# A decoder layer in float32 on one core: branch and output projections as seven block products of eight, in one stream with the MLP

## The chip, the core and the metric

The kernel runs on one core of a Trainium2 chip. The time is device microseconds (us) of one execution. The engines are TensorE (PE, matrix products into the eight PSUM banks), VectorE (DVE), ScalarE (ACT), GpSimd (POOL) and SyncE (SP, which here issues most of the transfers between HBM and SBUF). Each engine works through its own instructions in order and waits on semaphores for the others.

## What is computed

One layer of a decoder on x of 1024 tokens by 1024 features, all in float32. Cut to what matters here:

```python
h = rms_norm(x, norm_mix_g)
# three branches from projections of h, each 1024 features wide:
#   y_m: matrix memory, y_d: differential attention, y_c: cross-attention into 256 memory tokens
g_m, g_d, g_c = split(sigmoid(h @ w_gate + b_gate))
merged = g_m * (y_m @ w_proj_m) + g_d * (y_d @ w_proj_d) + g_c * (y_c @ w_proj_c)
x = x + merged @ w_out
h2 = rms_norm(x, norm_mlp_g)
x = x + square(relu(h2 @ w_up)) @ w_down        # 1024 -> 4096 -> 1024
```

## The kernel before

**Products.** Everything on the chip is kept with features on the partitions and the 1024 tokens along the row. A float32 operand is split into a rounded high part and the rest (`split`, `split2`: a copy on ACT that rounds, then a subtraction on DVE), and a product is three matmuls, high by high, high by low and low by high (`mm3`). So one product of 128 x 128 weights with 512 tokens is three matmuls of 512 columns.

**Stages.** `run` computes the three branches and the sigmoid gates (`gate_steps`; the gate products are used to fill PE while branch work waits), and stores the branch outputs (`store_y`, in `yd`) and the gates to HBM. Then `tail` runs three stages:

1. *Branch projections*, for branches c, m and d: `k_tiles` loads the branch output as eight tiles of 128 features and splits them; for each of four groups of 256 output features `group` runs 2 x 2 tiles x 8 steps x 3 = 96 matmuls. `merge` multiplies each result tile by its gate and adds it to the sum over branches (on POOL for the second branch).
2. *Output projection*: the same `group` four times on the merged tiles. `res` adds x, stores the new x, adds up the squares for the next norm (POOL), and stores the scaled tile for the next stage.
3. *Up projection* (`wino`), and then `down`: these already work with block products. Weights and operand are cut in quarters (two feature halves by two output halves for the weights, two feature halves by two token halves for the operand). Seven products of sums of quarters (`PROD`) stand in for eight products of quarters.

**A unit of block products.** Take 256 output features and all tokens. For each of the four steps of 256 input features, seven `mm3` go into seven PSUM banks: 4 x 7 x 3 = 84 matmuls. The weights of a step come in as four quarters; POOL makes four sums (`wino_s`, L1124 to L1127), ACT and DVE split all seven (`wsp`, tile `wo`, L104 and L105). The operand's sums are made by `wino_t` (L1106 to L1109, three on DVE and one on POOL) and split into a tile of seven blocks (`xo`, or `xd` in the down projection). At the end of the unit `combine` adds the seven PSUM banks up to the four result tiles (L1179 to L1185, on DVE), and `use_up` finishes them. The next unit's first product goes to the eighth bank, the others into banks as `combine` empties them.

**Order.** In these stages the instructions of PE, DVE and ACT are kept in program order (`InOrder`, `pinned`); the weight split of a step is issued two to three steps ahead of its products. A wait at the head of an engine's queue holds everything behind it. Where nothing is pinned, the framework's planner orders the instructions by its own estimates.

**Changes of stage.** The up projection starts with a special order, `runs`: its first unit is computed in two halves around the second. The down projection has its own pools, and 28 accumulators; there four operand tiles stay in SBUF and each pass takes one new.

## Time and profile before

| | us |
|---|---|
| runs (three) | 2285.44, 2285.45, 2289.59; median 2285.45 |
| span of the profiled execution | 2287.7 |
| PE busy | 2203.0 (96% of the span) |
| DVE busy | 1388.2 (61%) |
| ACT busy | 1012.3 (44%) |
| POOL busy | 543.9 (24%) |

The profile comes from an execution of its own. Its span runs from the first to the last instruction; the page gives no other time for that execution. Busy shares are averages over stages that have different limits: the branches run to about 1193 us, the rest of the gates to about 1286, the branch projections to 1547, the output projection to 1640, the up projection to 1953 and the down projection to the end. So each stage is read by itself.

### The profile page before, as it was taken

The page shows a single profiled execution, that of the slowest core. Times are in us where ns is not written, and L with a number is a line of the kernel's source. Part 1 is how long each engine was busy: PE and PEld are TensorE (multiplying, and loading weights), DVE is VectorE, ACT ScalarE, POOL GpSimd, SP SyncE. Part 2 cuts the span into 40 slices and gives each one's busy share as a digit, 9 for nine tenths or more (in the row PEclk, how much of TensorE's full clock was granted, in tenths as well). Part 3 has the DMA queues.
Part 4 walks back from the last instruction along what each step waited for, and adds up shares of the span by engine and source line. Part 5 has one row for each costly group of instructions (what it writes and reads, how often), then busy time and mean ns, then how long its engine had stood idle before and what let it go on. Part 6 is the DMA issues. An engine that isn't in the chain of part 4 may idle for free.

```text
span 2287.7 us, 30578 instructions
## 1 busy us (share of the span) xinstructions
PE 2203.0 (96%) x11222; PEld 1884.3 (82%) x11222; DVE 1388.2 (61%) x2627; ACT 1012.3 (44%) x1994; POOL 543.9 (24%) x696
## 2 busy tenths in 40 slices
PE   7999999999999999999899999999999999899998
PEld 5788789888898999999787888887787888688777
DVE  6636457552147777777652123454598777856678
ACT  6533445543246666666453112223445444543332
POOL 2100000000011111111000002201576665565553
PEclk9999999999999999999999999999999999999999
DMA  6023212201311110011134225435525444844434
GB/s 242 19 79 102 88 44 83 83 24 62 98 58 33 38 37 24 19 38 33 42 113 168 101 90 174 134 115 173 195 99 204 152 153 148 319 164 152 139 128 166
DMA packets 113781, 247.90 MB, mean 108 GB/s; under 512 B 11065, under 2 KB 19550, under 8 KB 111582
## 3 DMA queue, kind: packets, MB, share of 16 engines
q1 hardware_dynamic: 111326, 233.36, 30.4%
q10 hardware_dynamic: 2304, 12.58, 1.3%
q8 instruction: 88, 1.44, 0.3%
q14 instruction: 63, 0.52, 0.1%
HBM read 178.76 MB, written 67.14 MB: 107 GB/s over the span
## 4 chain that ended last, share of the span: by engine, by line
PE 70%; DVE 14%; DMA 7%; ACT 5%; issue 3%; POOL 2%; SPq 0%; ACTq 0%; DVEq 0%; POOLq 0%
PE mm L91 43%; PE p L91 18%; PE sc L91 4%; ACT dpe L987 2%; PE po L91 2%; DVE sc L979 1%; PE tp L94 1%; DMA wraw<-in_wdown 1%; DMA raw<-in_wd 1%; DVE wo L105 1%; DVE w L112 1%; DVE dpe L1000 1%; DVE daT L112 1%; DVE dq L867 1%; DMA raw<-in_wgate 1%
## 5 line engine op out<-in xcount | busy, mean ns | idle before, releaser
L91 PE MATMUL mm<-w,hT 128*128 128x384 f32 (+3 forms) x2496 | 474.0, 331 | 13.7 <-DVE dq L867 9.0
L91 PE MATMUL mm<-hT,w 128*128 128x512 f32 x1920 | 471.0, 400 | 8.2 <-ACT w L111 5.2
L91 PEld LDWEIGHTS mm<-hT,w 128*128 128x128 f32 x1920 | 360.1, 191 | 84.9 <-ACT w L111 5.8
L91 PEld LDWEIGHTS mm<-w,hT 128*128 128x128 f32 x2496 | 387.4, 189 | 33.3 <-DVE dq L867 13.7
L91 PE MATMUL p<-xd,wo 128*128 128x512 f32 x1344 | 314.1, 395 | 16.2 <-DVE acc L1543 8.5
L91 PEld LDWEIGHTS p<-xd,wo 128*128 128x128 f32 x1344 | 253.9, 190 | 76.3 <-DVE acc L1543 12.4
L91 PE MATMUL p<-xo,wo 128*128 128x512 f32 x1344 | 307.5, 390 | 3.2 <-DVE st L1397 1.8
L91 PEld LDWEIGHTS p<-xo,wo 128*128 128x128 f32 x1344 | 251.4, 188 | 57.9 <-ACT pt L1210 2.2
L112 DVE TENSOR_TENSOR w<-raw,w 128x256 fp32r<-128x256 f32 (+3 forms) x304 | 172.9, 589 | 162.4 <-ACT w L111 161.2
L91 PE MATMUL mm<-kt,w 128*128 128x512 f32 x1152 | 261.3, 389 | 0.0
L91 PEld LDWEIGHTS mm<-kt,w 128*128 128x128 f32 x1152 | 216.2, 188 | 45.0 <-DVE w L112 0.2
L111 ACT CAST w<-raw 128x256 fp32r<-128x256 f32 (+3 forms) x304 | 154.3, 532 | 193.5 <-PE mm L91 112.8
L104 ACT CAST wo<-wraw 128x896 fp32r<-128x896 f32 x122 | 114.8, 942 | 187.7 <-PE p L91 121.9
L105 DVE TENSOR_TENSOR wo<-wraw,wo 128x896 fp32r<-128x896 f32 x122 | 146.2, 1213 | 51.3 <-ACT wo L104 51.1
L1124 POOL TENSOR_TENSOR wraw<-wraw 128x128 f32<-128x128 f32 x128 | 100.9, 788 | 207.3 <-DMA wraw<-in_wdown 132.5
L987 ACT ACTIVATE dpe<-sc,dst,drr 128x256 f32<-128x256 f32 (+7 forms) x128 | 106.6, 833 | 94.0 <-DVE dst L983 92.0
L105 DVE TENSOR_TENSOR xd<-xd 128x1536 fp32r<-128x1536 f32 (+2 forms) x36 | 69.2, 1929 | 69.4 <-ACT xd L104 69.3
L979 DVE CUSTOM_DVE_ANT_0 sc<-sc,tmask 128x256 f32<-128x256 f32 (+7 forms) x128 | 96.9, 757 | 16.5 <-PE sc L91 16.5
L1125 POOL TENSOR_TENSOR wraw<-wraw 128x128 f32<-128x128 f32 x128 | 100.9, 788 | 0.0
L127 POOL TENSOR_SCALAR drr<-drr 128x16 f32<-128x16 f32 x16 | 3.6, 222 | 397.4 <-DVE drr L935 397.4
L1126 POOL TENSOR_TENSOR wraw<-wraw 128x128 f32<-128x128 f32 x128 | 90.7, 708 | 0.0
L127 POOL TENSOR_SCALAR hss<-hss 128x4 f32<-128x4 f32 x8 | 3.3, 409 | 356.2 <-ACT mscr L747 237.6
(319 smaller groups left out, 3084.9 us busy)
## 6 DMA issues: line engine op xcount, KB each, us to landing
wraw<-in_wup SPq DMA_DIRECT2D x64, 256.0 KB, 3.1
r_d<-xts SPq DMA_DIRECT2D x16, 1024.0 KB, 4.2
wraw<-in_wdown SPq DMA_DIRECT2D x64, 256.0 KB, 2.8
xd<-r_d SPq DMA_DIRECT2D x19, 768.0 KB, 6.9
xd<-r_d SPq DMA_DIRECT2D x14, 1024.0 KB, 5.9
raw<-in_wgate SPq DMA_DIRECT2D x48, 256.0 KB, 2.8
gates<-gt SPq DMA_DIRECT2D x48, 256.0 KB, 2.0
raw<-in_wd SPq DMA_DIRECT2D x32, 384.0 KB, 3.2
```

Of the source, the lines that this page charges most:

```text
L91: self.pin(self.nc.tensor.matmul(out, l, r, start=start, stop=stop))
L94: self.pin(self.nc.tensor.transpose(out, x, self.ident))
L104: self.A.copy(hi, src)
L105: self.V.tensor_sub(lo, src, f32(hi))
L111: nc.scalar.copy(hi, src)
L112: nc.vector.tensor_sub(lo, src, f32(hi))
L867: V.scalar_tensor_tensor(out=qT[lo, c], in0=pt[lo], scalar=self.gd[lo], in1=f32(qT[lo, c]), op0=ALU.mult, op1=ALU.subtract)
L979: V.tensor_tensor_reduce(out=sc[:, 0:n], in0=sc[:, 0:n], in1=self.tmask[:, D - n : D], scale=1.0, scalar=-3.0e38, op0=ALU.add, op1=ALU.max ...
L987: nc.scalar.activation(pe[c][:, 0:n], sc[:, 0:n], AF.Exp, bias=t8[:, 2 + c : 3 + c], scale=rr[:, i, c : c + 1], accum_out=t8[:, 4 + c : 5 ...
L1124: G.tensor_add(r[:, 4], r[:, 0], r[:, 3])
L1125: G.tensor_sub(r[:, 5], r[:, 4], r[:, 1])
L1126: G.tensor_sub(r[:, 6], r[:, 1], r[:, 0])
```

## The change

The branch projections and the output projection become units of the kind that the up projection has. Units 0 to 3 are branch c, 4 to 7 branch m, 8 to 11 branch d, 12 to 15 the output projection and 16 to 31 the up projection; 128 steps of four to a unit run in one loop, and `down` goes on with the same rings: two weight tiles of two steps each (`w_load`, `w_sum`), three split weight tiles (`w_split`), five operand tiles X (four in `down`). The special order at the start of the up projection is gone.

The operand's block sums of the branch outputs are made while the branches run: `keep_y` stores the quarters, and `finish_y` makes four sums in place on POOL and stores them. For branch c, `cross` does this from HBM during branch m. Operand tiles then come ready from HBM and only need the split. The first three, and the first weights, are loaded and split while the last gates run.

The merge of a branch now works on the four result tiles of a unit, with a running sum that goes to HBM and back (`pd`) between the branches. The operands of the output and up projections are made from the unit just finished; one in four goes through HBM (`od`, `ud`). In one loop, all of DVE, ACT and POOL are kept in program order. The list `early` holds what is issued ahead of a step's weight work, `late` what follows it, and `switch` sets these for a change of branch.

The diff, cut to its core:

```diff
+    def quarters(self, b, t):
+        V, G = self.V, self.G
+        G.tensor_sub(t[:, 0], b[:, 2], b[:, 0])
+        V.tensor_sub(t[:, 1], b[:, 0], b[:, 1])
+        V.tensor_sub(t[:, 2], b[:, 2], t[:, 1])
+        V.tensor_sub(t[:, 3], b[:, 3], t[:, 2])
...
+    def finish_y(self, b, kp, t):
+        self.quarters_in_place(t)
+        self.nc.sync.dma_start(self.yx[b][kp, :, 3:7], t)
...
+        def cross(kp):
+            y = pool.tile([P, 4, 512], F32, tag="yc", name=self.name("ycq"))
+            nc.sync.dma_start(y[:, 0], self.yc0[kp])
+            nc.sync.dma_start(y[:, 1:4], self.yx[2][kp, :, 0:3])
+            self.finish_y(2, kp, y)
...
+        for kp in range(4):
+            add(170 + 90 * kp, cross, kp)
...
+    def w_side(self, n):
+        self.w_split(n + 2)
+        if n % 2:
+            self.w_load((n + 5) // 2)
+        else:
+            self.w_sum(n // 2 + 2)
...
+            def use_branch(u, cs):
+                bi, g = divmod(u, 4)
+                t = gt[u]
+                for i in (1, 3, 2, 0):
+                    V.scalar_tensor_tensor(out=t[:, i], in0=t[:, i], scalar=1.0, in1=cs[i], op0=ALU.add, op1=ALU.mult)
+                    if bi:
+                        G.tensor_add(bt[u][:, i], bt[u][:, i], t[:, i])
+                yield
+                if bi < 2:
+                    A.dma_start(self.pd[g], bt[u] if bi else t)
+                else:
+                    t_make(u)
+                yield
+            def use_out(u, cs):
...
+                for i in (1, 3, 2, 0):
+                    V.scalar_tensor_tensor(out=x[:, i], in0=cs[i], scalar=0.5, in1=x[:, i], op0=ALU.mult, op1=ALU.add)
...
+                t_make(u)
+                for i in range(4):
...
+                        A.activation(q, x[:, i], AF.Square)
+                        G.tensor_add(ssq[:, s], ssq[:, s], q)
+                yield
...
+            def switch(N, i, srcs):
+                s = lambda k: (i + k) % 5
+                if 0 in srcs:
+                    LA(N - 13, lambda: self.x_load(i, s(0), srcs[0]))
+                    LA(N - 10, lambda: sp_(i, 0))
+                    LA(N - 9, lambda: sp_(i, 1))
+                if 1 in srcs:
+                    LA(N - 4, lambda: self.x_load(i + 1, s(1), srcs[1]))
+                    LA(N - 2, lambda: (sp_(i + 1, 0), sp_(i + 1, 1)))
...
+            for N, i, u, d in ((48, 12, 8, self.od), (64, 16, 12, self.ud)):
+                LA(N - 11, lambda u=u, i=i: make(u, i, i % 5, (0,)))
+                LA(N - 10, lambda u=u, i=i: make(u, i, i % 5, (1,)))
+                EA(N - 6, lambda u=u, d=d: keep(u + 1, d))
+                switch(N, i, {1: d})
+                LA(N - 2, lambda u=u, i=i: make(u + 2, i + 2, (i + 2) % 5, (0, 1)))
+                LA(N + 1, lambda u=u, i=i: make(u + 3, i + 3, (i + 3) % 5, (0, 1)))
...
+            for n in range(128):
+                u, kp = divmod(n, 4)
...
+                for j, (l, q) in enumerate(self.PROD):
+                    self.mm3(ps[j], (w[:, l, 0], w[:, l, 1]), (x[:, q, 0], x[:, q, 1]), kp == 0, kp == 3)
...
+                for f in early.pop(n, []):
+                    f()
+                self.w_side(n)
+                for f in late.pop(n, []):
+                    f()
+                if kp == 3:
+                    cs = self.combine(ps, True)
+                    g = (use_branch if u < 12 else use_out if u < 16 else use_up)(u, cs)
+                    step = lambda g=g: next(g, None)
+                    for k in range(3):
+                        early.setdefault(n + 1 + k, []).insert(0, step)
...
-            self.tail()
+                        self.tail_open(ct)
+                        tasks = self.tail_tasks()
+                        for i, _ in enumerate(self.gates):
+                            if i % 6 == 1:
+                                next(tasks, lambda: None)()
+                        for f in tasks:
+                            f()
+            self.tail(ct)
...
-    nc = bacc.Bacc("TRN2", target_bir_lowering=False, num_devices=1)
+    nc = bacc.Bacc("TRN2", target_bir_lowering=False, num_devices=1, dynamic_dma_scratch_size=1024)
```

The weights of the four projections are laid out in quarters on the host, as those of the MLP were. `split2` is used for all splits of the stream.

769 lines of the change are left out of this document (328 added, 441 removed).

## The prediction

> **What bounds the kernel now.** I read the page first: span, busy shares, chain of waits.
>
> ```profile
> span 2287.7 us, 30578 instructions
> PE 2203.0 (96%) x11222; PEld 1884.3 (82%) x11222; DVE 1388.2 (61%) x2627; ACT 1012.3 (44%) x1994; POOL 543.9 (24%) x696
> ...
> PE 70%; DVE 14%; DMA 7%; ACT 5%; issue 3%; POOL 2%; SPq 0%; ACTq 0%; DVEq 0%; POOLq 0%
> ...
> L91 PE MATMUL mm<-kt,w 128*128 128x512 f32 x1152 | 261.3, 389 | 0.0
> ```
>
> TensorE (PE) is the bound, and the three branch projections (the last row) are its cleanest stretch: 1152 matmuls in 261.3 us with no idle time, so a matmul of 512 columns costs 261.3/1152 = 0.2268 us of PE. The 389 ns is one matmul's latency; they overlap. Next, when the stages start and end, by tile, and how busy each engine is in some stretches (columns: length, then busy time and count of PE, PEld, DVE, ACT, POOL, the granted clock, DMA).
>
> ```profile
> L91 PE MATMUL mm<-kt,w x1152: 388/389/411, 1286.4 to 1547.3; 128*128 128x512 f32 x192
> L91 PE MATMUL p<-xo,wo x1344: 387/389/505, 1639.9 to 1953.1; 128*128 128x512 f32 x192
> L91 PE MATMUL p<-xd,wo x1344: 387/389/797, 1953.3 to 2283.3; 128*128 128x512 f32 x192
> ```
>
> ```profile
> 1547.50:1639.90 92.40, 89.29 (x385) 73.08 (x385) 39.23 (x38) 32.23 (x42) 25.82 (x20) 0.98 0.57 189
> 1639.90:1953.30 313.40, 310.17 (x1378) 255.21 (x1377) 257.10 (x304) 152.78 (x218) 201.34 (x267) 1.00 0.45 160
> 1940.00:1990.00 50.00, 42.58 (x166) 33.01 (x165) 42.01 (x40) 27.71 (x31) 25.46 (x30) 0.91 0.87 314
> 1655.00:1700.00 45.00, 45.00 (x208) 37.57 (x207) 44.56 (x55) 20.92 (x29) 38.17 (x47) 1.00 0.28 99
> 1245.00:1560.00 315.00, 315.00 (x1385) 260.61 (x1385) 111.50 (x133) 62.73 (x75) 28.21 (x29) 1.00 0.36 120
> ```
>
> By these rows the output projection takes 92.4 us for 384 matmuls (87.1), so it loses 5.3; the up projection takes 313.4 for 1344 (304.8), 8.6 over. In 1940 to 1990, at the change to the down projection, 166 matmuls ran where 50/0.2268 = 220 fit: 12.3 us lost. Two more things count below. While the branches are projected VectorE (DVE) is busy 111.5 of 315 us: there is room. From 1655 to 1700 it is busy 44.56 of 45 us with GpSimd (POOL) at 38.17, and PE still loses nothing: that is how full the pair can be.
>
> **What is removed.** A projection group goes from 96 matmuls to 4 x 7 x 3 = 84 (a unit), in 16 groups: 192 matmuls, 192 x 0.2268 = **-43.5 us**. All of it is on the path, as PE is. A unit then lasts 84 x 0.2268 = 19.05 us. The separate starts of the output and up stages go too: -5.3, and of the 8.6 what the 32 small matmuls of the row statistics don't use.
>
> ```profile
> L91 PE MATMUL px<-dg,ones 128*128 128x128 f32 x16 | 2.1, 274 | 0.0
> L91 PE MATMUL px<-ones,ssq 128*128 128x1 f32 x16 | 1.8, 245 | 0.0
> ```
>
> They stay (3.9), so -4.7.
>
> **What is added, and on which engines.** Each unit of projection now does what a unit of the up projection does: four weight splits (w_split, one DVE subtraction of 896), the seven adds out of PSUM (combine), eight POOL operations of 256 (w_sum). In use_branch and use_out come four operations of 512 whose inputs are both in SBUF, as combine leaves its results there. Units 4 to 11 add four POOL adds of 512, units 8 to 15 the block sums (three of 512 on DVE, one on POOL), units 12 to 15 up to four POOL adds for the row statistics. And each operand tile X is split once: 1536 and 2048 on DVE. Prices, first of DVE and POOL alone, then where they meet:
>
> ```profile
> L105 DVE TENSOR_TENSOR wo<-wraw,wo x122: 1075/1196/1377, 1651.9 to 2273.9; 128x896 fp32r<-128x896 f32 x122
> L112 DVE TENSOR_TENSOR xo<-xr,xo x4: 1746/1754/2009, 1591.0 to 1660.1; 128x1536 fp32r<-128x1536 f32 x4
> L112 DVE TENSOR_TENSOR xo<-xts,xo x4: 2279/2339/2542, 1593.3 to 1663.3; 128x2048 fp32r<-128x2048 f32 x4
> L1328 DVE TENSOR_TENSOR gl<-mg,gl x16: 691/692/943, 1485.9 to 1548.5; 128x512 f32<-128x512 f32 x16
> L1326 POOL TENSOR_TENSOR mg<-mg,gl x16: 1282/1284/1298, 1394.2 to 1461.5; 128x512 f32<-128x512 f32 x16
> ```
>
> ```profile
> 1681.61 3.67 DVE L1214 TENSOR_TENSOR pt<-pt,p 128x512 f32<-128x512 f32 x6
> ...
> 1687.08 0.94 DVE L1179 TENSOR_TENSOR pt<-pt,pt 128x512 f32<-128x512 f32 x1
> 1687.95 0.94 DVE L1108 TENSOR_TENSOR xts<-rq,xts 128x512 f32<-128x512 f32 x1
> 1688.81 0.95 DVE L1180 TENSOR_TENSOR pt<-pt,pt 128x512 f32<-128x512 f32 x1
> ...
> 1693.56 0.68 DVE L1184 TENSOR_TENSOR pt<-pt,pt 128x512 f32<-128x512 f32 x1
> 1694.17 0.68 DVE L1183 TENSOR_TENSOR pt<-pt,pt 128x512 f32<-128x512 f32 x1
> ```
>
> ```profile
> 1682.41 0.46 POOL L1125 TENSOR_TENSOR wraw<-wraw 128x128 f32<-128x128 f32 x1
> 1682.94 0.46 POOL L1127 TENSOR_TENSOR wraw<-wraw 128x128 f32<-128x128 f32 x1
> 1683.36 1.30 POOL L1107 TENSOR_TENSOR xts<-rq 128x512 f32<-128x512 f32 x1
> ...
> 1687.44 0.90 POOL L1125 TENSOR_TENSOR wraw<-wraw 128x128 f32<-128x128 f32 x1
> 1688.42 0.79 POOL L1127 TENSOR_TENSOR wraw<-wraw 128x128 f32<-128x128 f32 x1
> ```
>
> ```profile
> 1807.83 0.69 DVE L1106 TENSOR_TENSOR xts<-rq 128x512 f32<-128x512 f32 x1 [0.74 <-ACT rq L1383]
> 1808.56 1.67 DVE L1108 TENSOR_TENSOR xts<-rq,xts 128x512 f32<-128x512 f32 x1
> ```
>
> Read them so. While DVE adds out of PSUM (1681.61, six in 3.67 us, 0.61 each) POOL runs at its own speed (0.46 and 1.30). When DVE has both inputs in SBUF and POOL works too, they take turns: DVE starts one every 0.87 us (1687.08, 1687.95, 1688.81) where alone it starts one every 0.61 (1693.56, 1694.17), so a POOL operation of 128 costs DVE 0.26. One of 512 costs 1.10: the two DVE operations from 1807.83 to 1810.23 take 2.40 where 0.61 + 0.69 would do. On the line between, one of 256 costs 0.54 (an estimate; two of 128 would be 0.52). Starts follow 0.08 us closer than the shown durations (0.69 against 0.61), so 896 counts 1.00, and a tile X 1.67 + 2.20 = 3.87.
>
> The Trainium skill, page "SBUF — State Buffer", section "Who interferes with whom", says that a DVE instruction with two SBUF inputs contends with a GpSimd instruction that reads SBUF, and that the loser fully blocks. It speaks against this change, which puts just such work on both. That they exclude each other the rows bear out; that a whole profiled duration is blocked they don't: 0.69 + 0.46 = 1.15 would be the step, and it is 0.87. What the sum would be by it is among the rivals.
>
> DVE's time in a unit, without X: 7 x 0.61 + 4 x 0.61 + 4 x 1.00 = 10.7. POOL charges it 8 x 0.54 = 4.3, and 1.10 for each operation of 512. Some of that lies beneath the PSUM adds: in the stretch at 1681.61 POOL filled 2.7 of 3.67 us, so I let three quarters of 4.3 (3.2) hide; the bounds are all and none.
> - Units 0 to 3: 10.7 + 4.3 - 3.2 = 11.8, with X at most 17.4. PE hides it.
> - Units 4 to 7 (X: 6.1, 3.9, 0, 5.5): 10.7 + 8.7 - 3.2 = 16.2. Over 19.05 by 3.2, 1.0, 0, 2.7.
> - Units 8 to 11 (X: 6.1, 3.9, 0, 7.7): 12.5 + 9.8 - 3.2 = 19.1. Over by 6.2, 4.0, 0.1, 7.9.
> - Units 12 to 15 (X: 3.9, 3.9, 0, 7.7): the same, 2.2 less in unit 12. Over by 1.7, 3.9, 0.1, 7.8.
> - Unit 16, with the remains of 15 and one X: 3.9. Later up units have no more than before: nothing.
>
> Together 42.5. The weight ring enters two steps (9.5 us) ahead; I count half of that as cover, so **+38 us**. All hidden: 25; none hidden: 80.
>
> **Smaller terms.** The fourth X of the first stage can load only when the gates have left their memory; it is needed 3 x 4.76 = 14.3 us later.
>
> ```profile
> DMA to landing us min/median/max: 4.4/6.6/13.7
> L1384 ACTq DMA_DIRECT2D r_d<-rq x16: 326/327/348, 1681.1 to 1966.4; - x16
> POOL wraw L1124 <- DMA wraw<-in_wup: 63.9, 24, 19.2
> ```
>
> X tiles (xd, first row) land in 4.4 to 13.7 us, and split plus ACT copy take some 6: between 0 and 6, I take **+3**. At the change to the down projection X 20 loads early, but 21 to 23 still stand with the last combine in DVE's queue (3 x 3.87 + 4.3 + 2.4 + 1.8 = 20 us), and the weight split of step 130 behind them has 9.5 us: of the 12.3 lost now I take **-5** (0 to -12). In the branches POOL does 48 block sums of 512 in place (cross, finish_y): 48 x 1.10 = 53 us of DVE at most, of which the chain of waits has 14%: 0 to 7, **+4**. The hss and drr statistics queue behind up to four of them (5.1 us) and are wanted a chunk later. On ACT's queue a store of pd waits for POOL's adds, and the next weight cast stands behind it; this is inside the excess, since that cast feeds DVE. ACT's 32 more issues of 0.33 lie in its idle 56%. On SP the finish_y stores wait for POOL with weight loads behind them: hidden by loads a group ahead, else the 5 us of one finish each.
>
> Sum: 2287.7 - 43.5 - 5.3 - 4.7 + 38 + 3 - 5 + 4 = **2274.2** for the profiled execution. The page gives no time beside its span, and the runs' median, 2285.45, lies 2.3 below it, so I predict **2272**.
>
> **Rivals.**
> - The pair does not bind (its excess is absorbed by the rings): 38 becomes 0, 2236 or 2234 in the runs. For it: 1655 to 1700, DVE full, PE whole. Against: there the work of both just fitted; here twelve units in a row exceed it, and rings of two or three tiles carry no more than 10 us.
> - **Slower**: POOL blocks DVE for its whole duration (0.73 for 256, 1.28 for 512, from 0.46 and 1.28). Each unit from 4 on gains some 2.3 us, the excess is 71 - 5 = 66: 2302, in the runs 2300. With nothing hidden beneath the adds, because POOL then waits for its weights (63.9 us of such waits now), 80: 2314. It decides from an excess of 43.5 + 5.3 + 4.7 + 5 - 3 - 4 = 51.5. For it: DVE is in order, and X splits stand ahead of weight splits. Against: the step of 0.87. The skill's sentence on full blocking is this rival.
> - No change: an excess of 47 to 56, for instance because the three X loads at a change of branch land late (13.7 us) and hold DVE's queue some 5 us at each of two changes: 2283 and up.
>
> **Chances.** Forecast (excess 25 to 47) 0.38; not bound 0.17; no change 0.15; slower 0.30. No change means within 0.2% (4.6 us), about what a measurement tells apart. Faster 0.55, same 0.15, slower 0.30. The range runs from a little above the unbound case to near "nothing hidden": 2240 to 2312; the forecast's own is 2257 to 2280.
>
> **What would show it.** Units 0 to 3 near 19.05 us each, without idle PE; units 4 to 7 near 21, 8 to 15 near 23, with PE waiting for DVE (combine, weight split) and DVE over 95% busy there; up units at 19.05 again; under 12 us lost at the start of the down projection; branches before 1286 as now. It is wrong if units 8 to 15 keep 19.05, if PE waits there for DMA instead, or if the branches are over 7 us longer.

## The result and the profile after

The changed kernel takes 2389.86 us (median of 4 runs, 2386.07 to 2390.72) against 2287.52 for the kernel before in the same series (2285.44 to 2293.31): a ratio of 1.0435, 95% interval 1.0409 to 1.0461. The forecast was 2272, its range ended at 2312. The profiled execution took 2386.07, its span 2384.1, so the difference to explain is 2384.1 - 2287.7 = 96.4 us.

The page of the changed kernel first: span, busy shares, the matmuls of the stream (both projections and the whole MLP are one group now) and the weights' block sums on POOL.

```profile
span 2384.1 us, 29987 instructions
PE 2212.2 (93%) x11030; PEld 1862.6 (78%) x11030; DVE 1585.5 (67%) x2747; ACT 1058.3 (44%) x2015; POOL 672.0 (28%) x635
...
L80 PE MATMUL p<-x,wo 128*128 128x512 f32 x4032 | 976.0, 403 | 87.6 <-DVE wo L56 25.2
...
L56 POOL TENSOR_TENSOR wraw<-wraw 128x256 f32<-128x256 f32 x376 | 379.0, 1030 | 538.1 <-DMA wraw<-in_wup 159.0
```

PE has 11030 matmuls in place of 11222, the 192 that the change removes, and yet it is busy 9 us longer and stands 87.6 us ahead of matmuls of the stream. By tile, the first row gives the start of the stream; the second is the copy with which ScalarE opens each unit's combine, 32 in all. The difference of two starts of that copy is taken below as the length of a unit; where the copy is late in ACT's queue and PE is not, one unit looks longer and the next shorter.

```profile
L80 PE MATMUL p<-x,wo x4032: 387/393/797, 1308.8 to 2379.3; 128*128 128x512 f32 x192
L56 ACT COPY u<-p x32: 567/579/587, 1324.3 to 2051.8; 128x512 f32<-128x512 f32 x32
```

The stream begins at 1308.8, where the first branch product began at 1286.4: **+22.4** before the first product that the change touches. The down projection begins near 2055.7, so 32 units take 746.9 where branches, output and up projections took 666.9: **+80**. The down projection and the end take 328.4 against 334.4: **-6**. Together 96.4.

A unit without idle PE would be 19.05 us. Units 1 to 3 took 67.4 (10 over), units 4 to 17 372.7 (**106 over**, of which unit 17 alone, which took 35.7, has 17), units 18 to 30 262.5, 20.2 each (15 over), unit 31 24.9 (6 over). The stretches of the changed kernel, units 4 to 7, 8 to 11, 12 to 15, 16 and 17, and 18 to 30, then units 4 to 17 as a whole (length, then busy time and count of PE, PEld, DVE, ACT and POOL, granted clock, DMA share, GB/s):

```profile
1391.70:1487.10 95.40, 83.28 (x336) 63.92 (x336) 71.88 (x68) 29.67 (x30) 47.69 (x44) 0.96 0.64 233
1487.10:1588.60 101.50, 86.65 (x336) 66.06 (x336) 90.05 (x77) 31.33 (x30) 70.21 (x50) 0.93 0.54 189
1588.60:1699.20 110.60, 90.10 (x336) 67.99 (x336) 89.40 (x81) 42.39 (x47) 65.70 (x51) 0.88 0.43 148
1699.20:1764.50 65.30, 50.38 (x183) 38.98 (x183) 41.07 (x49) 21.53 (x29) 26.19 (x23) 0.82 0.24 84
1764.50:2026.90 262.40, 255.35 (x1095) 203.88 (x1094) 200.86 (x235) 117.00 (x172) 105.73 (x117) 1.00 0.40 145
...
1391.64:1764.38 372.74, 310.29 (x1189) 236.87 (x1190) 292.40 (x273) 124.87 (x132) 209.79 (x165) 0.90 0.48 170
```

The last row is the one to read twice. In units 4 to 17 **no engine is full**: PE 83%, DVE 78%, POOL 56%, ACT 34%, DMA 48%. DVE, which the prediction held to be the bound, stands for 80 of the 372.7 us. What PE waits for in 1380 to 1765 (us in total, times, longest):

```profile
PE p L80 <- DVE wo L56: 17.2, 16, 3.4
PE p L80 <- DVE c L56: 13.8, 7, 4.4
PE p L80 <- ACT u L56: 12.3, 4, 5.1
PE p L80 <- ACT wo L56: 10.3, 6, 5.9
```

And DVE and ACT in the same stretch, their largest waits:

```profile
DVE wo L56 <- ACT wo L56: 50.1, 18, 6.7
```

```profile
ACT wo L56 <- POOL wraw L56: 66.8, 12, 11.6
ACT wo L56 <- PE p L80: 39.2, 8, 12.7
ACT b L56 <- issue: 35.5, 3, 12.7
ACT wo L56 <- POOL b L56: 29.4, 4, 9.1
ACT q L56 <- POOL ssq_rb L56: 21.2, 10, 6.1
```

PE waits for a weight split (wo on DVE) or for a combine (u on ACT, c on DVE); DVE's weight split waits for ACT's cast; ACT's cast waits for POOL's sums, or for an instruction ahead of it in ACT's queue. The chain has one more link, outside these engines. In the same stretch POOL's sums wait for the weight loads, 106 us over the four weight tensors, half of it for those of branch m (the row below). On SP's queue, which issues these loads, a weight load waits until DVE's split has freed the raw weight tile, of which there are two (121.6 us), and the gate loads ahead of it for POOL's adds (91.3 us). Such a wait is a loss only where the sums then come late: in units 18 to 30 POOL waits for weight loads 127.8 us, and PE stands 7.

```profile
POOL wraw L56 <- DMA wraw<-in_wpm: 52.1, 5, 12.1
```

One unit of this, the change from unit 15 to 16, in the timelines of DVE, ACT and PE (start, us, in brackets the idle time before and its releaser):

```profile
1691.16 2.44 DVE L56 TENSOR_TENSOR wo<-wraw,wo 128x896 fp32r<-128x896 f32 x2 [6.67 <-ACT wo L56]
1693.52 3.95 DVE L56 TENSOR_TENSOR x<-x 128x1536 fp32r<-128x1536 f32 x2
1697.39 2.30 DVE L56 TENSOR_TENSOR x<-b,x 128x1536 fp32r<-128x1536 f32 x1
1699.62 2.82 DVE L56 TENSOR_TENSOR x<-t,x 128x2048 fp32r<-128x2048 f32 x1
1702.36 1.61 DVE L56 TENSOR_TENSOR wo<-wraw,wo 128x896 fp32r<-128x896 f32 x1
1703.89 0.67 DVE L56 TENSOR_TENSOR c<-u,p 128x512 f32<-128x512 f32 x1
...
1715.40 1.46 DVE L56 TENSOR_TENSOR wo<-wraw,wo 128x896 fp32r<-128x896 f32 x1 [2.54 <-ACT wo L56]
```

```profile
1689.67 0.63 ACT L56 ACTIVATE q<-g 128x512 f32<-128x512 f32 x1 [1.37 <-POOL ssq_rb L56]
1690.21 1.76 ACT L56 CAST wo<-wraw 128x896 fp32r<-128x896 f32 x2
...
1699.08 0.57 ACT L56 COPY u<-p 128x512 f32<-128x512 f32 x1
1712.34 1.15 ACT L56 ACTIVATE b<-g,vec 128x1024 f32<-128x1024 f32 x1 [12.69 <-issue]
...
1714.44 0.93 ACT L56 CAST wo<-wraw 128x896 fp32r<-128x896 f32 x1
```

```profile
1691.18 1.22 PE L80 MATMUL p<-x,wo 128*128 128x512 f32 x2 [5.90 <-ACT wo L56]
...
1704.62 11.53 PE L80 MATMUL p<-x,wo 128*128 128x512 f32 x38 [3.96 <-DVE c L56]
```

Read it downward. ACT squares for the row statistics and waits for POOL to free the tile of squares (1.37); the two weight casts behind the square start at 1690.21, so DVE, which stood 6.67, and PE, which stood 5.90, go on at 1691.2. Then DVE splits X for 9 us; ACT has opened the combine at 1699.08, but DVE comes to it only at 1703.89, and PE stands 3.96 for a bank. Now ACT stands 12.69 (the row names no releaser; DVE makes g, from which b is made, from 1709.04 to 1712.86); only then does it make b, and behind b the next weight cast at 1714.44, for which DVE has stood 2.54 by 1715.40. At each moment one engine works for the others.

Unit 17 is long for a reason of its own. Its work holds the row statistics of the MLP's norm, and in ACT's fixed order the copy of the row factor stands until PE has made it; the next weight casts, at 1754.77, are behind that copy and what follows from it:

```profile
1744.43 0.59 ACT L56 COPY ssq_rb<-px 128x512 f32<-128x512 f32 x1 [15.15 <-PE px L80]
```

In the kernel before the two such copies stood 0 and 2.34 us.

### The profile page after: what moved, and what is told of

It reads as the page before. It is cut to its first block, busy times and chain, and to the rows that moved or that the text cites. A ratio compares the mean times of both kernels' runs of the same rounds, so it can differ in the third digit from the quotient of the medians.

```text
span 2384.1 us, 29987 instructions
## 1 busy us (share of the span) xinstructions
PE 2212.2 (93%) x11030; PEld 1862.6 (78%) x11030; DVE 1585.5 (67%) x2747; ACT 1058.3 (44%) x2015; POOL 672.0 (28%) x635
## 5 line engine op out<-in xcount | busy, mean ns | idle before, releaser
L80 PE MATMUL p<-x,wo 128*128 128x512 f32 x4032 | 976.0, 403 | 87.6 <-DVE wo L56 25.2
L80 PEld LDWEIGHTS p<-x,wo 128*128 128x128 f32 x4032 | 770.7, 193 | 291.3 <-DVE wo L56 41.0
L56 POOL TENSOR_TENSOR wraw<-wraw 128x256 f32<-128x256 f32 x376 | 379.0, 1030 | 538.1 <-DMA wraw<-in_wup 159.0
L56 DVE TENSOR_TENSOR wo<-wraw,wo 128x896 fp32r<-128x896 f32 x190 | 238.2, 1263 | 191.5 <-ACT wo L56 181.3
L56 DVE TENSOR_TENSOR x<-x 128x1536 fp32r<-128x1536 f32 (+1 forms) x60 | 129.3, 2161 | 20.1 <-ACT x L56 20.0
L56 DVE TENSOR_TENSOR u<-u,p 128x512 f32<-128x512 f32 x160 | 107.1, 686 | 14.1 <-DVE u L56 0.9
L56 ACT CAST x<-x 128x1536 fp32r<-128x1536 f32 (+1 forms) x60 | 101.0, 1691 | 15.3 <-DMA x<-y 14.3
L56 DVE TENSOR_TENSOR acc<-acc,p 128x512 f32<-128x512 f32 x100 | 67.2, 685 | 30.3 <-PE p L80 29.4
L80 PEld LDWEIGHTS po<-dv,daT 128*128 128x128 f32 x576 | 75.6, 193 | 13.8 <-DVE daT L101 12.3
L80 PE MATMUL po<-dv,daT 128*128 128x256 f32 x576 | 78.4, 280 | 7.0 <-DVE daT L101 6.9
```

Of the source, the lines that this page charges most:

```text
L56: return self.tc.keep_in_program_order(f(*a, **k))
L80: self.pin(self.nc.tensor.matmul(out, l, r, start=start, stop=stop))
```

## The experiments

All kernels below are the changed one with the edit shown. Unit lengths are read as above. Each of e1 to e15 was run once, e16 four times. The kernel before took 2282 to 2295 us in these comparisons, so the stretches inside one profile decide rather than differences of a few us in the whole. How well a stretch repeats is seen where the edit lies ahead of the stream (e4, e7, e10, e15): units 4 to 17 took 370.6 to 376.1 there, units 18 to 30 261.7 to 262.7. The table collects what was measured: the time, the start of the first branch product, the length of the two groups of units, and the share of units 4 to 17 in which VectorE is busy.

| kernel | us | first product | units 4-17 | units 18-30 | DVE busy in 4-17 |
|---|---|---|---|---|---|
| changed | 2389.86 | 1308.8 | 372.7 | 262.5 | 78% |
| e1 adds on VectorE | 2371.08 | 1312.3 | 359.6 | 257.1 | 82% |
| e2 weight split first | 2380.51 | 1307.1 | 375.8 | 252.9 | 77% |
| e3 weight sums left out | 2341.17 | 1308.6 | 335.4 | 259.4 | 81% |
| e4 cross placed later | 2384.66 | 1307.1 | 373.0 | 262.2 | 78% |
| e5 no GpSimd | 2330.62 | 1307.5 | 328.9 | 255.0 | 81% |
| e6 stores on SyncE | 2379.65 | 1310.6 | 368.0 | 262.1 | 81% |
| e7 cross pinned | 2408.57 | 1326.5 | 376.1 | 261.7 | 78% |
| e8 e5 and no splits of X | 2298.67 | 1311.0 | 300.8 | 254.4 | 71% |
| e9 combine first | 2417.01 | 1309.5 | 390.8 | 275.9 | 71% |
| e10 no early sums | 2363.13 | 1285.8 | 372.2 | 261.7 | 79% |
| e11 lead of three | 2448.42 | 1310.8 | 396.8 | 295.0 | 75% |
| e12 e1, e9 and e11 | 2353.81 | 1308.8 | 345.5 | 262.4 | 85% |
| e13 two of three matmuls | 2378.53 | 1314.0 | 371.6 | 264.1 | 79% |
| e14 e12, weight sums on VectorE | 2439.45 | 1306.6 | 373.0 | 309.1 | 83% |
| e14b e1, e2 in up, sums on VectorE | 2429.14 | 1312.9 | 384.8 | 284.0 | 80% |
| e15 cross in the last branch | 2380.58 | 1304.6 | 370.6 | 262.7 | 79% |
| e16 e12 and e15 | 2344.49 | 1307.1 | 341.9 | 260.5 | 86% |

**Is it the pair of VectorE and GpSimd?** The first theory is the prediction's slower rival: the two engines keep each other off SBUF for longer than was counted.

```diff
-        G.tensor_sub(t[:, 0], b[:, 2], b[:, 0])
+        V.tensor_sub(t[:, 0], b[:, 2], b[:, 0])
...
-                        G.tensor_add(bt[u][:, i], bt[u][:, i], t[:, i])
+                        V.tensor_add(bt[u][:, i], bt[u][:, i], t[:, i])
...
-                        G.tensor_add(ssq[:, s], ssq[:, s], q)
+                        V.tensor_add(ssq[:, s], ssq[:, s], q)
```

> The changed kernel with 70 operations of 512 moved from GpSimd to VectorE: the 32 adds of the branch sum, the 24 first block sums of a result and the 14 adds for the row statistics. All else as in the changed kernel (span 2384.1 us; units 4 to 17 take 373 us). Theory 1, the shared port: such an operation costs VectorE 1.10 us while GpSimd does it and 0.61 when VectorE does it, so units 4 to 17 get shorter, by 20 to 40 us. Theory 2, VectorE simply has too much to do in order and GpSimd is no hindrance: 70 x 0.61 = 43 us more on VectorE, so longer by up to 40 us.

Measured: units 4 to 17 13 us shorter, the up units 5 (their one POOL operation of 512 per unit moved too). The sign is that of theory 1, the pair; the size is below its 20.

```diff
-        if i < len(self.wsrc):
+        if i < 2:
             r, G = self.raws[i], self.G
```

> The changed kernel without the weight sums on GpSimd (the four sums of each weight pair are made only for the first two pairs and what they left is used for all others; the weight loads and splits stay). Theory 1, the shared port: GpSimd's charge on VectorE falls by 4.3 us in every unit, so units 4 to 17 get some 50 us shorter and the up units go to 19.1 (15 us). Theory 3, queue order: the splits still stand behind the finishing of a unit; the up units stay near 20 and units 4 to 17 gain less than 20.

Measured: 37 us off units 4 to 17, between the two theories, and 3 off the up units, as theory 3 said. The edit takes away POOL's meetings with DVE and also the wait of ACT's cast for the sums, so the 37 are not contention alone. Both edits of e1 and e3 together:

> Both edits of before together: the 70 operations of 512 (branch adds, first block sum, sums of squares) on VectorE, and the weights' block sums left out after the first two pairs (the tiles of the first pairs stand in, so the products of the later weights are wrong numbers; loads, splits and matmuls stay). GpSimd has next to nothing to do in units 4 to 17. Those took 372.8 us in the changed kernel, 359.7 with the operations moved, 335.5 with the sums left out; 266.7 without an idle TensorE. Theory A (VectorE and GpSimd hold each other up, and this is the excess): the two gains add up or more, 4 to 17 at 322 or less, the whole at 2328 or less. Theory B (what is left is the order of the queues, the splits of X ahead of the combine, and VectorE's own work): the 70 operations are simply more work for VectorE, 4 to 17 stay at 333 to 350, the whole at 2339 to 2357.

Measured: 328.9, between the two theories; the gains (13 and 37) come to 44 together, less than their sum. The window of units 4 to 17 in that kernel shows DVE still idle 62 us with POOL out of the way:

```profile
1388.22:1717.13 328.91, 293.51 (x1189) 229.23 (x1190) 267.23 (x328) 125.46 (x132) 1.85 (x2) 0.94 0.53 190
```

So POOL's work is a part of the 106 us, and not the larger one: with all of it gone from POOL 62 stay. (VectorE has the moved operations to do in e5; what the stretch would take without them was not run.) ACT's casts, which wait for the weight loads themselves once the sums are gone, stood 9.7 us for them in e5 in 1380 to 1720; a third raw weight tile was not tried. What a meeting costs can be read from one operation, DVE's weight split, in the changed kernel and then in e5 (groups with shapes kept apart, 1388 to 1762):

```profile
L56 DVE TENSOR_TENSOR wo<-wraw,wo 128x896 fp32r<-128x896 f32 x56 | 81.5, 1468 | 50.7 <-ACT wo L56 47.4 <-issue 3.2
```

```profile
L56 DVE TENSOR_TENSOR wo<-wraw,wo 128x896 fp32r<-128x896 f32 x64 | 68.8, 1087 | 34.6 <-ACT wo L56 33.9
```

1.468 against 1.087. Over all of DVE's work in units 4 to 17: 292.4 busy in the changed kernel; in e5 267.2, of which the 328 - 273 = 55 moved operations are 55 x 0.69 = 38; 292.4 - (267.2 - 38) = 63 us of contention.

**Weights ahead of the unit's other work.** In each step w_side was called after the pieces of work kept in `early`; here before them.

```diff
-                for f in early.pop(n, []):
-                    f()
-                self.w_side(n)
+                self.w_side(n)
+                for f in early.pop(n, []):
+                    f()
```

> The changed kernel with only the order of issue changed: in each step the weight work stands ahead of the steps that finish the unit before. Theory 3, queue order (the weight copy on ScalarE and its subtraction on VectorE stand behind the finishing of a unit and come too late for TensorE): the up units go from 20.2 to about 19.1 us (15 us in all), the units 4 to 17 gain 20 us or more. Theory 1, the shared port: the work is the same, so units 4 to 17 change by less than 8 us in all, and the up units stay at 20.2.

Measured: up units 252.9, 10 us shorter, units 4 to 17 3 us longer (no more than the spread above). So the 15 us of the up units are for two thirds the order of ScalarE's and VectorE's queues: the cast for the next weights stood behind ReLU and square of the last unit.

**Stores.** ScalarE's queue issues the stores of the stream, and a store waits for its data.

```diff
-                A.dma_start(d[:, 0:3], bt[u][:, 1:4])
+                nc.sync.dma_start(d[:, 0:3], bt[u][:, 1:4])
... (the same for the other five stores of the stream)
```

> All stores of the stream issued by SyncE's queue in place of ScalarE's. Theory A (a store that waits for VectorE's last block sum holds ScalarE's queue, and with it the copy that opens the next combine): units 4 to 17 shrink by 20 us or more, the whole at 2366 or less. Theory B (ScalarE only waits for what it would wait for anyway): units 4 to 17 within 8 us of 372.8, the whole at 2378 to 2394. Theory C (on SyncE's queue the waiting stores hold back the loads of X and of the weights): longer than 2394.

Measured: 368.0, 5 us shorter: theory B. At most these 5 us of ScalarE's idle time are the stores'.

**The splits of X.** e5, and the splits left out from the sixth input on:

```diff
         t = self.X[i]
-        self.split2(t[:, s, 0], t[:, s, 1], f32(t[:, s, 1]))
+        if not 5 <= i < 20:
+            self.split2(t[:, s, 0], t[:, s, 1], f32(t[:, s, 1]))
```

> As the kernel without GpSimd's work in the loop (operations of 512 on VectorE, weight sums left out after the first two pairs), and also without the splits of X after the first five inputs of products: the loads of X stay, TensorE multiplies by the tiles of earlier X, so the output is wrong numbers from there on. Theory A (the splits, which stand ahead of the next combine in VectorE's and ScalarE's queues, are the rest of the excess): units 4 to 17 at 267 to 285 us, the whole at 2270 to 2300. Theory B (the rest is the gates, block sums, stores and sums of squares, which stay): units 4 to 17 at 300 or more, the whole over 2305.

Measured: 300.8, 28 us less than e5, and 2298.67 for the whole: by the stretch theory B, by the whole theory A. Neither holds alone: the splits are 28 of the 62 us that e5 has over its matmuls, 34 stay. Most of those lie in unit 8 (28.8 us, 9.7 over) and in units 16 and 17 (54.3, 16.2 over; the copy of the row factor stands 12.99 us there).

**Order alone.** The combine is issued ahead of the splits that stood before it.

```diff
+                if kp == 3:
+                    cs = self.combine(ps, True)
+                    ... (the steps of the unit's further work, as before)
                 for f in early.pop(n, []):
                     f()
                 self.w_side(n)
                 for f in late.pop(n, []):
                     f()
-                if kp == 3:
-                    cs = self.combine(ps, True)
-                    ...
```

> Only the order in the queues: after the last product of a unit, combine is issued ahead of the weight split and of the splits of X that stood before it. Nothing is left out. VectorE is busy only 292 of the 372.8 us of units 4 to 17 in the changed kernel. Theory A (order: TensorE stands because combine, which frees its banks, is behind X splits that wait for ScalarE and DMA; it waits 26 us there for u and c): those waits go, units 4 to 17 at 355 or less, the whole 2369 or less. Theory B (work: the two engines have so much to do that any order is late): within 8 us of 372.8, 2378 to 2394; the waits move from u and c to wo.

Measured: 390.8, 18 us longer, and the up units 13 longer. Neither was expected. PE's waits for u fell from 12.3 to 1.5 us and for c from 13.8 to 9.1, as theory A said, but they moved to wo, as theory B said: what had been put first made the next thing late.

```profile
PE p L80 <- ACT wo L56: 24.4, 7, 7.9
PE p L80 <- DVE wo L56: 22.7, 23, 3.5
```

**Lead alone.**

```diff
-            w = self.wop[m % 3].tile([P, 7, 2, P], F32R, tag="wo", name=self.name("wo"))
+            w = self.wop[m % 4].tile([P, 7, 2, P], F32R, tag="wo", name=self.name("wo"))
...
-        self.w_split(n + 2)
+        self.w_split(n + 3)
```

To make room the squares of the row statistics go to combine's tiles, so in units 12 to 15 the edit is not lead alone; in the up units no squares are added up.

> The weight split is issued three products ahead in place of two, in a ring of four weight tiles in place of three, as the up projection had it before. To make room, the row sums of squares share their tile with the row factors, and the squares go to the tiles of combine in place of one of their own. Nothing is left out. Theory A (the chain ScalarE cast, VectorE split, behind GpSimd's sums is late by latency; another product of lead, 4.76 us, covers it): TensorE's waits for wo go, up units 18 to 30 at 247 to 252 us in place of 262.5, units 4 to 17 at 350 or less, the whole at 2350 or less. Theory B (the engines lack time, and a ring only fills once): up units 257 or more, 4 to 17 at 363 or more, the whole at 2375 or more.

Measured: 396.8, and 295.0 in the up units: 24 and 32 us longer, the opposite of theory A. PE's waits for wo are gone from the list of 1380 to 1765; in their place:

```profile
PE p L80 <- ACT u L56: 60.1, 12, 7.4
```

The sums on POOL keep their place, so a cast three products ahead comes one product sooner after them. ACT's casts wait for them 203.3 us in place of 66.8 in 1380 to 1765, and 47.6 in the up units, where they had not waited at all; the copy that opens the combine is behind the cast in ACT's queue. All three edits (e1, e9, e11) together:

> Three edits of before together: weight split three products ahead in a ring of four, combine ahead of the splits, and the 70 operations of 512 on VectorE. Nothing is left out. If latency and order are what the units lack (VectorE busy 78% there), the gains add up: units 4 to 17 at 300 to 330 us, up units at 248 to 253, the whole at 2300 to 2340. If it is work, units 4 to 17 stay at 345 or more and the whole at 2355 or more.

Measured: 345.5 and 2353.81. By the stretch this is theory B (the whole lies between the two); but two edits that cost 18 and 24 us alone save 14 with the third (359.6 with e1 alone), and DVE's share rises to 85%. The edits are not terms of a sum.

**What sets the pace?** In units 0 to 17 each product issues two of its three matmuls; all that VectorE, ScalarE, GpSimd and the queues do stays.

```diff
-                    self.mm3(ps[j], (w[:, l, 0], w[:, l, 1]), (x[:, q, 0], x[:, q, 1]), kp == 0, kp == 3)
+                    if n < 72:
+                        for c, (e, f) in enumerate(((0, 0), (1, 1))):
+                            self.mm(ps[j], w[:, l, e], x[:, q, f], start=kp == 0 and c == 0, stop=kp == 3 and c == 1)
+                    else:
+                        self.mm3(ps[j], (w[:, l, 0], w[:, l, 1]), (x[:, q, 0], x[:, q, 1]), kp == 0, kp == 3)
```

> In units 0 to 17 each product issues two of its three matmuls (the correction of the weights' low part by the inputs' high part is left out, and the inputs' low part goes with the weights' low part, so the output is wrong numbers); everything around the matmuls stays. A unit's matmuls are then 12.7 us in place of 19.05. Theory A (the chain ScalarE, VectorE, GpSimd sets the pace of units 4 to 17, and TensorE only waits for it): they stay at 335 us or more. Theory B (TensorE's own time is in the sum: stalls add to it, and its half clock after stalls is what stretches them): 372.8 less a third of the 270 us of matmuls, 270 to 300. In units 18 to 30, which are as in the changed kernel, both expect 20.2 each.

Measured: 371.6 where it was 372.7. The window of units 4 to 17:

```profile
1383.14:1754.74 371.60, 255.71 (x805) 180.81 (x806) 292.98 (x275) 124.68 (x132) 220.83 (x169) 0.80 0.48 174
```

A third of the matmuls (1189 to 805, by 0.2268 us each 87 us) is gone and the stretch is 1.1 us shorter; DVE, ACT and POOL did the same work in the same time. In units 4 to 17 the other engines set the pace and **TensorE's own time is not part of it**. This is theory A, and it says at once what the saved matmuls that lie there (12 in each of units 4 to 15, 144 of the 192) were worth: nothing. In units 1 to 3 of e13, where PE stands little, the missing matmuls do count: 57.4 us in place of 67.4.

**The same without GpSimd, and nothing left out.** e12 with the weight sums on VectorE, one product later in its queue; and the same with the changed kernel's order and lead (with the order of e2 in the up units).

```diff
-            r, G = self.raws[i], self.G
+            r, G = self.raws[i], self.V
...
         if n % 2:
             self.w_load((n + 5) // 2)
-        else:
-            self.w_sum(n // 2 + 2)
+            self.w_sum((n + 3) // 2)
```

> As the run with three edits (lead of three, combine ahead, the 70 operations of 512 on VectorE: 2353.8), and the weights' block sums on VectorE too, one product later in the queue so that their loads have landed. GpSimd has no work left in units 4 to 17; nothing is left out. The sums are 4 operations of 256 for every two products, by an estimate from VectorE's 0.61 for 512 some 0.35 us each, so 2.8 us of VectorE in a unit, 39 in units 4 to 17. Theory A (hand-overs to a slower third engine and its port are the loss): units 4 to 17 at 325 or less (345.5 in the run with three edits), the whole at 2336 or less. Theory B (VectorE lacks the time): 350 or more, the whole 2358 or more.

> The same with the order and the lead of the changed kernel (split two products ahead, ring of three, combine last; in the up units the weight split ahead of the unit's other work): the 70 operations and the weight sums on VectorE, nothing left out. Theory A: units 4 to 17 at 335 or less (359.7 with the 70 operations alone moved, 328.9 with the sums left out as well), up units near 19.2 each, the whole at 2340 or less. Theory B: 360 or more, 2368 or more.

Measured: 373.0 and 384.8, by the numbers theory B both times. The window of units 4 to 17 of the first:

```profile
1380.63:1753.62 372.99, 310.27 (x1219) 238.60 (x1218) 310.10 (x442) 124.36 (x133) 1.84 (x2) 0.90 0.49 175
```

No POOL, so no contention, and the same 373 us as the changed kernel. But that VectorE lacks the time, as theory B has it, is not shown: it is idle 63 us here, and in the up units of the same run, which grew to 309.1, it is busy 220.8. The sums also have another place in the order, and in the lead of three the cast of a pair's first product now follows them in the same step: ACT's casts waited 102.9 us for them in these up units.

**The branches.** First the four `cross` calls placed later in the planner's list (262 + 70 kp in place of 170 + 90 kp).

```diff
-            add(170 + 90 * kp, cross, kp)
+            add(262 + 70 * kp, cross, kp)
```

> The changed kernel with the block sums of branch c moved from positions 170, 260, 350, 440 of branch m to 262, 332, 402, 472. The changed kernel reaches its first block product at 1308.8 us, 22.4 later than the kernel before. If these loads and sums stand in the way of the small chain of transfers of the gates of branch m (about 220 to 256 us), some 15 us of the 22 come back. If the block sums of branches m and d slow the branches as such, less than 5 comes back.

Measured: first product 1307.1; but the planner ran all four between 193 and 250 us as before, so it tells nothing. With GpSimd's operations there and its row statistics kept in the order of the program:

```diff
-        G = self.nc.gpsimd
+        G = InOrder(self.tc, self.nc.gpsimd)
         G.tensor_sub(b[:, 1], b[:, 0], b[:, 1])
```

> The four re-loads of the cross branch and their block sums placed at 262 + 70 kp on GpSimd in the order of the program, so that they cannot run between 188 and 262 us, beside the chain of small transfers of the memory gates; nothing left out. In the run before this one the planner moved them back there although they were placed late. Theory A (that bunch beside the gates' chain is the loss ahead of the first branch product): the first branch product at 1287 to 1295 us instead of 1308.8, the whole at 2366 to 2376. Theory B (the loss comes from the other stores, sums and waits of the branches): at 1304 or later, the whole at 2380 to 2392.

Measured: 1326.5, 18 us later than the changed kernel. The bunch has left 188 to 262 us, and PE lost in 340 to 500 instead: 874 matmuls ran there, where 993 ran in the changed kernel. Leaving the early sums out altogether (the stream loads stored blocks a second time in their place):

```diff
     def finish_y(self, b, kp, t):
-        self.quarters_in_place(t)
-        self.nc.sync.dma_start(self.yx[b][kp, :, 3:7], t)
+        return
...
-            add(170 + 90 * kp, cross, kp)
```

> The early block sums of the branch outputs are left out (finish_y and cross issue nothing; the first stage of the stream loads stored blocks a second time in their place, three loads for each input in place of two, so the output is wrong numbers). The stores of the blocks stay, in their new tiles. Before, the first branch product began at 1286.4 us, in the changed kernel at 1308.8. Theory A (the sums, their stores and the re-loads of the cross branch are the loss): at 1284 to 1292, the whole at 2363 to 2374. Theory B (the loss lies elsewhere: the tiles of four blocks kept until the last is made, or the loads of the stream): at 1300 or later, the whole at 2376 to 2392.

Measured: 1285.8, theory A; its tile row:

```profile
L80 PE MATMUL p<-x,wo x4032: 387/393/796, 1285.8 to 2356.6; 128*128 128x512 f32 x192
```

The early sums with their transfers are the whole +22. And their place:

```diff
                 if i == 3:
                     self.finish_y(1, kp, y)
+                    y = pool.tile([P, 4, 512], F32, tag="y", name=self.name("ycq"))
+                    nc.sync.dma_start(y[:, 0], self.yc0[kp])
+                    nc.sync.dma_start(y[:, 1:4], self.yx[2][kp, :, 0:3])
+                    self.finish_y(2, kp, y)
```

> The changed kernel with the four re-loads and block sums of the cross branch made in the last branch, one after each of its own four, where the planner cannot draw them ahead; nothing left out. Without any early sums the first branch product began at 1285.8 us, in the changed kernel at 1308.8. Theory A (most of the 23 us is the bunch beside the gates' small transfers, in 188 to 262 us, where TensorE lost 12): the first branch product at 1297 or earlier, the whole at 2374 or less. Theory B (GpSimd's in-place sums cost much the same wherever they stand): 1303 or later, 2380 or more.

Measured: 1304.6, 4 us earlier, and 2380.58: by the numbers theory B, that the sums cost much the same wherever they stand. The windows 188 to 262 of the kernel before, the changed one and e15:

```profile
188.00:262.00 74.00, 71.20 (x397) 62.06 (x398) 37.71 (x121) 28.89 (x81) 0.00 (x0) 0.95 0.24 71
```

```profile
188.00:262.00 74.00, 59.11 (x319) 51.45 (x319) 39.45 (x102) 19.30 (x52) 21.30 (x16) 0.87 0.52 166
```

```profile
188.00:262.00 74.00, 67.85 (x388) 59.05 (x387) 37.02 (x119) 27.54 (x77) 0.00 (x0) 0.98 0.24 69
```

Of 397 matmuls before, 319 and then 388 ran in the window: the bunch of cross (21.3 us of POOL, twice the DMA share) does cost there, 12 us of PE's busy time. What it holds up is seen in PE's waits of the changed kernel, a transposition of the memory gates that waits for a chain of small transfers:

```profile
255.85 0.31 PE L545 MATMUL tp<-ident,g_b 32*128 32x32 f32 x1 [10.40 <-ACT g_b L526]
```

In the kernel before it ran at 238.96 after 1.60 us of waiting, 16.9 earlier. The last branch (its first product, sc<-dk,dq) began at 666.5 in the kernel before, at 685.6 in the changed one and at 669.9 in e15. So 19.1 of the 22.4 us are lost before the last branch, and e15 gets 15.7 of them back; but its first product of the stream gains only 4.2 on the changed kernel. Moved into the last branch, the sums cost most of it there. Which of their parts costs there, POOL against DVE or the transfers (4 x 1 MB in, as much out), was not separated.

**The best version.** e12 with e15, nothing left out:

> The run with three edits (the 70 operations of 512 on VectorE, combine ahead, the weight split three products ahead) and the cross branch's re-loads and block sums in the last branch. Nothing is left out. If the gains add: 2353.8 less 4, 2346 to 2354, a ratio of 1.024 to 1.029 to the kernel before. If the sums moved into the last branch collide with VectorE there as they did alone: 2354 to 2362. Nobody expects it under 2300: units 4 to 17 would still have 70 us or more over their matmuls.

Measured over repeated runs: 2344.49 us against 2292.06, a ratio of 1.0228 (1.0211 to 1.0245). It wins some 45 us back, a little more than was expected, and stays slower than the kernel before; units 4 to 17 are still 75 us over their matmuls, and the first product 20.7 late.

```profile
1381.98:1723.85 341.87, 295.26 (x1206) 230.86 (x1205) 293.61 (x329) 125.04 (x133) 131.72 (x114) 0.93 0.53 189
```

No version with nothing left out is faster than the kernel before. A mixture, the seven-product form in some stages only, was not tried.

## Why the prediction was wrong

**What bounds.** That PE bounded the kernel before was right, and the -43.5 us are really off PE: 192 matmuls fewer. The step that failed is the next one, that this is "on the path, as PE is". The change itself took PE off the path: by e13, PE's time is no part of units 4 to 17, so 144 of the 192 matmuls were saved where nothing waits for them.

**The term of +38**, the excess of units 4 to 16, is the step that failed most: units 4 to 16 have 89, and unit 17, which was put at nothing, 17 more. Its working was "DVE's time in a unit", over 19.05 or not. That work was sized well. For units 4 to 15 the prediction's list makes 80.3 + 94.1 + 89.7 = 264 us of DVE, the windows show 71.9 + 90.1 + 89.4 = 251. The charge of POOL on DVE, 73 us in the same list, measures 57 in these units by the reckoning above (251.2 in the changed kernel, 228.8 in e5 with 50 moved operations). The bounds beside the +38, 25 and 80, come to about 27 and 75 when the list is redone with the same cover off both; nothing hangs on that. What was wrong is the turn from work to time: it supposed that DVE is always busy while it is late, "over 95% busy", and it was 75, 89 and 81% in units 4 to 15 and 63% in 16 and 17. Through the rings of two and three tiles, the weight load, POOL's sum, ACT's cast, DVE's split and the combine stand in one chain, each in an order fixed beforehand, so a late link lets the others stand. In every kernel of the table DVE stayed between 71 and 86% of units 4 to 17.

**The start of the up stage** (-4.7) did not go; it moved into units 16 and 17, which have 27 us over their matmuls. Unit 17 has 17 of these, and in the row above ACT stands 15.15 in it for the row statistics. In e8, without POOL's work and the splits of X, unit 17 still took 32.0. That the wait for the row factor makes most of this is read from the order of the rows; no run takes it out. What became of the start of the output stage (-5.3) cannot be told from the rest of units 12 to 15.

**The cover of 5 us** by the weight ring was of the wrong kind: in e11 one more product of lead for the cast, without its sums, makes the stretch longer.

**Units 0 to 3** were to have "near 19.05 us each"; units 1 to 3 took 21.2, 18.3 and 27.9, 10 us over, where +3 was counted for the fourth X of the first stage. That X cost PE nothing: PE's matmuls run without a wait from 1308.79 to 1351.88. The loss is in unit 3, at the change of branch: ACT waits for the load of an X of the next branch, the copy that opens the combine is behind that X's cast in ACT's queue, and PE stands for the combine. In e8, without these casts, units 1 to 3 took 58.7, in e5, which has them, 65.2:

```profile
1390.27 1.47 ACT L56 CAST x<-x 128x1536 fp32r<-128x1536 f32 x1 [4.49 <-DMA x<-y]
```

```profile
1392.28 1.65 PE L80 MATMUL p<-x,wo 128*128 128x512 f32 x3 [4.59 <-ACT u L56]
```

This is what the "no change" rival had named, late loads at a change of branch; the forecast itself had no term for it.

**"Later up units have no more than before: nothing"** failed by 15 us. Their work is the same, but in another order and with a lead of two in place of three; e2 gives 10 of them back by order alone.

**The branches** (+4, at most 7) cost +22.4, and e10 shows that the early sums are all of it. The sizing took 48 sums by 1.10 us of DVE by DVE's 14% of the chain of waits. The sums met something else, the memory gates' chain of small transfers, beside which the planner put all four re-loads; placed elsewhere (e7, e15) they cost nearly as much or more there, and why is open. A move "past each queue" was priced by an average share, and an average says nothing of the one place where the work lands.

**The down projection** (-5) gave -6 as a stage, and that this is near is luck. Its opening, where less than 12.3 us was to be lost, lost more: in 2040 to 2090 of the changed kernel 129 matmuls ran, 50 - 129 x 0.2268 = 20.7 us lost. Of the stage alone, the first 36 us lost 16.1 (89 matmuls in 36.3) where 12.4 were lost before (107 in 36.7); the gain came later in the stage, where the prediction had none, and its cause is open.

```profile
2040.00:2090.00 50.00, 33.99 (x129) 25.44 (x129) 35.22 (x35) 24.20 (x28) 14.96 (x14) 0.83 0.84 314
```

**The rivals.** "The pair does not bind" is out. The slower one had the right sign and the wrong mechanism: it needed POOL to block DVE for its whole duration and came to 2300 to 2314; contention measures less than the prediction's own price, and with POOL's work gone 62 of the 106 us stay (e5). Of "no change", the late loads are there (the loss in unit 3, and 13.4 us in which ACT's x waits for DMA in 1380 to 1765), as a small part. The signs that it named for being wrong came true in one of three: the branches were over 7 us longer. That units 8 to 15 would take 23 us with PE waiting for combine and weight split was right about what PE waits for (in 1380 to 1765 31 us for wo and c on DVE, 22.6 for ACT's part of the same chain), and wrong in length: 25.4 and 27.7.

What stays open: how the 106 us divide among the links. The weight sums are 37, the moved adds 7 to 13, the splits of X 28, the rest 34, but these are what leaving out returns in one order, and e9, e11 and e12 show that the same edit has either sign in another. Not tried were more raw weight tiles, sums moved ahead together with the casts, and the row factor taken out of ACT's way in unit 17.

## What to carry to other kernels

Before work is moved from TensorE to engines that feed it, ask for their hand-overs and not only for their busy time: in this kernel, where ScalarE, VectorE and GpSimd pass each tile on in a fixed order through rings of two or three, VectorE never got beyond 86% of units 4 to 17, so there its work had to be divided by about 0.8 before it was compared with TensorE's. That is what these orders reached and no limit of the engine: from 1655 to 1700 of the kernel before it was busy 44.56 of 45 us. Here a change that saved 12% of the matmuls in a unit and filled VectorE beyond that share lost. And work hidden in an earlier stage is priced at the place where the planner puts it, by what waits there, not by an average share.

## What the runs showed of the hardware that was not expected

The granted clock of TensorE fell to 0.90 in units 4 to 17, and nothing shows that this cost time: 1189 matmuls took 310.3 us of PE where 1189 x 0.2268 = 270 would do, and in e13, at 0.80, the stretch was as long. A lower clock beside idle PE is there a symptom and no cause of the length.

A DVE and a POOL operation that meet are both stretched. The weight split of 896 went from 1.087 to 1.468 us on average (rows above); POOL's sums of 256 in units 4 to 17 of the changed kernel, shortest, median and longest in ns:

```profile
L56 POOL TENSOR_TENSOR wraw<-wraw x110: 722/746/2778, 1387.9 to 1743.8; 128x256 f32<-128x256 f32 x110
```

Half of them run at their own speed, some nearly four times as long (spans on POOL are rough). The Trainium skill, page "SBUF — State Buffer", section "Who interferes with whom", says that a DVE instruction with two SBUF inputs contends with a GpSimd instruction that reads SBUF, and calls the ports that they share an exclusive lock; its words on full blocking stand beside the modes of DVE with two ports, and the prediction's rival took them for this case too. The trace agrees with contention: 63 us over units 4 to 17, where POOL was busy 209.8.

That PE's share (83%) is the highest of the stretch and PE is not its bound was not expected either. The Trainium skill, page "Perfetto Trace Analysis", section "Identifying the Most-Contended Engine", goes by occupancy to find the bottleneck, with the caution that a busy PE is no good measure; the share of weight loads is one of the figures that it takes for TensorE instead. By that (64% here) it would name VectorE with its 78%, yet e1, which gave VectorE more work, was 13 us shorter. In units 4 to 17 no occupancy tells it, and only the run with a third of the matmuls gone (372.7 to 371.6) tells which of them sets the time.
